# Retention values and gates of a head as a 2x2 block product with seven block products, weight sums by accumulating DMAs

## The chip, the cores and the metric

The kernel runs on one core of a Trainium2 chip. The metric is the device time of one execution in microseconds. A time is a median over runs of the same program; the profile is one further execution with the hardware profiler on.

## The reference, cut to what matters

One layer over 512 tokens with 1024 features, in float32. A normalised x is multiplied by one wide weight `w_in`; its columns are the inputs of two branches. Branch A (gated delta rule, 8 heads) is not touched. In branch B (retention, 4 heads) each head has 256 columns of queries and of keys and 512 columns of values `vb` and of gates `gb`:

```python
xn = rmsnorm(x, n_mix_pre)
proj = xn @ w_in
qa, ka, va, za, beta_logit, a_dt, qb, kb, vb, gb, gate_a, gate_b = _split_cols(proj, IN_SIZES)
...
ob = chunk_retention(qb, kb, vb)          # (q k^T * decay) v, per head
ob = rmsnorm(ob, norm_b) * silu(gb)       # per head, 512 columns
yb = ob @ w_br_b
mix = (sigmoid(gate_a) * ya + sigmoid(gate_b) * yb) @ w_out
x = x + rmsnorm(mix, n_mix_post)
x = x + rmsnorm(square(relu(rmsnorm(x, n_mlp_pre) @ w_up)) @ w_down, n_mlp_post)
```

So the values and gates of a head are one product: x (512 tokens by 1024 features) times two weight blocks of 1024 by 512.

## The kernel before, in words

Every product of float32 matrices is made of three matmuls on rounded operands, `mm3` (L78 to L83): a value is split into a rounded `hi` and a rest `lo`, and hi·hi, hi·lo and lo·hi are accumulated in one PSUM bank. x is split once, into the two tiles `xs`. Weights are split as they arrive: `weights` (L85 on) takes a block of 128 partitions by 1024 elements (two contraction tiles of 512 columns, 512 KB) by a DMA issued on SP into a tile `raw`, lets ScalarE cast it to `whi` (L100) and VectorE subtract to `wlo` (L101). `raw` has two buffers in the pool `ring`; after the first retention product two more in the pool `pb_` are used in turn (`raw_pools`). `whi` and `wlo` have three buffers each, so a block is split when the block three before it is done.

`feature_major` computes features by tokens, with weights stationary and x moving; `token_major` computes tokens by features, with x stationary and weights moving, in four PSUM banks of the tag `mm` (four banks in all), one for each 128 tokens. Each of its blocks feeds 24 matmuls.

For a head h, `retention(h)` loads a decay table (POOL), makes queries and keys and rotates them, makes the four score blocks, then the values with `token_major`, split into `vr`, and the output `o` in banks of the tag `dl`; sums of squares and `rsqrt` follow on small tiles. `gb_head` then makes the gates with `token_major`, and `gate_rows` applies tanh, a product and the row scale. After that comes a product of the branch weights with an earlier head's output: for h = 0 `ya_partial(3, ...)` and the gates of branch A into `acc`, for later heads `branch_partial` into `accb`. `gated_features` transposes `o` for the next head. After the loop the gates of branch B are applied in `accb`, and `mix` is formed from `accb` and `acc`.

The program is written in order, and a scheduler places each engine's instructions by priority and by when they are ready; the splits of weights have a higher priority (L99). Each engine and each DMA queue then executes in its own order, and waits where operands or buffers are not ready.

Of the kernel before, what the change touches and what calls it, by code (L numbers as in the profile page):

```python
# [15 lines left out]
ALU = mybir.AluOpType  # L16
# [44 lines left out]
def hybrid_block_kernel(ctx: ExitStack, tc: tile.TileContext, a: dict, out: bass.AP):  # L61
# [8 lines left out]
    raw_pools = [ring]  # L70
# [7 lines left out]
    def mm3(ps, lhs, rhs, first, last):  # L78
        lh, ll = lhs
        rh, rl = rhs  # L80
        nc.tensor.matmul(ps, lh, rh, start=first, stop=False)  # L81
        nc.tensor.matmul(ps, lh, rl, start=False, stop=False)  # L82
        nc.tensor.matmul(ps, ll, rh, start=False, stop=last)  # L83

    def weights(src, k0, nk, c0, ncols, keep=None):  # L85
# [3 lines left out]
        raw = raw_pools[i % len(raw_pools)].tile([P, 1024], F32, tag="raw", name="raw", bufs=2)  # L89
# [3 lines left out]
        )  # L93
        if keep is None:
# [4 lines left out]
        with tc.high_priority(200 if i >= 6 else 0):  # L99
# [5 lines left out]
        )  # L105

# [574 lines left out]
    with tc.tile_pool(name="pb", bufs=1) as pb_:  # L681
# [3 lines left out]
        accb = pb_.tile([P, 8, T], F32, name="accb")  # L685

        def rotary(pss, dst):
            r = [pb_.tile([P, T], F32, tag=f"ro{i}", name="ro") for i in range(4)]
# [10 lines left out]
        def retention(h):  # L699
            dec = pb_.tile([P, T], F32, tag="dec", name="dec")  # L700
            nc.gpsimd.dma_start(dec, a["c_decay"][h])
            qs, ks, vs = (
                [pb_.tile([P, n, T], F32R, tag=f"{nm}{i}", name=nm) for i in range(2)]
                for nm, n in (("qr", 2), ("kr", 2), ("vr", 4))
            )
# [3 lines left out]
            for i in range(4):  # L709
# [12 lines left out]
                sc = pb_.tile([P, T], F32, tag="sc", name="sc", bufs=2)  # L722
# [5 lines left out]
            pss = token_major(w_in, x_tile, OFF_VB + h * 512, 8)  # L728
            for t in range(4):
                nc.scalar.copy(vs[0][:, t, :], pss[t])  # L730
                nc.vector.tensor_tensor(vs[1][:, t, :], pss[t], vs[0][:, t, :], ALU.subtract)
            o = pb_.tile([P, 4, T], F32, tag="o", name="o")
            ss = pb_.tile([P, 4], F32, tag="oss", name="oss")
            sq = pb_.tile([P, T], F32, tag="osq", name="osq")
            for j in range(4):
# [11 lines left out]
                nc.scalar.activation(sq, ps, AF.Square, accum_out=ss[:, j : j + 1])  # L747
# [4 lines left out]
            return Rows(  # L752
                lambda t: [(o[:, t, :], rstd[:, t : t + 1], slice(0, T))],
                lambda t, f: o[:, t, f * P : (f + 1) * P],
            )

        def gb_head(h, rows):
            pss = token_major(w_in, x_tile, OFF_GB + h * 512, 8)
# [239 lines left out]
```

## Time and profile before

| | |
|---|---|
| median of 3 runs | 1408.81 us (1408.64 to 1409.47) |
| the profiled execution, its own time | 1407.76 us |
| its span, first to last instruction | 1406.1 us |
| TensorE busy | 1389.0 us (99%) |
| VectorE, ScalarE, GpSimd busy | 808.6, 571.6, 53.0 us |
| moved by DMA | 129.74 MB, mean 92 GB/s |

In the profile PE is TensorE's matmuls, PEld its weight loads, DVE is VectorE, ACT ScalarE, POOL GpSimd, SP SyncE; SPq and POOLq are the queues on which they issue DMAs. `mm<-whi,actT` reads: the tile `mm` written from `whi` (moving) and `actT` (stationary), where `actT` holds x. A matmul's listed duration overlaps the next one's. L101 is line 101 of the kernel.

### The profile page before, as it was taken

Reading aid. Unit: us, or ns where it says so; the run is one execution under the profiler, and the core shown is the slowest. Engines: PE = TensorE matmul, PEld = TensorE weight load, DVE = VectorE, ACT = ScalarE, POOL = GpSimd, SP = SyncE. Lnnn points to the kernel's source line nnn. Section 1 sums busy time; section 2 is a strip of 40 time slices with the busy share of each in tenths; the row PEclk is TensorE's granted clock in tenths of the full one; section 3 lists DMA queues with packets and bytes.
Section 4 is the critical chain, followed back from the end, with each engine's and each line's share of the span. In section 5 each row is a group of like instructions: output and inputs, shape, how many; then the busy total and the mean of one; then the engine's idle time right before and its main releaser. Section 6 shows DMA issues by size and latency. Waiting matters only on the chain.

```text
span 1406.1 us, 17493 instructions
## 1 busy us (share of the span) xinstructions
PE 1389.0 (99%) x6766; PEld 1140.7 (81%) x6766; DVE 808.6 (58%) x1463; ACT 571.6 (41%) x1082; POOL 53.0 (4%) x100
## 2 busy tenths in 40 slices
PE   8999999999999999999999999999999999999997
PEld 5888787878888888888888888888888888888886
DVE  5599889944755564536346455445685334344445
ACT  6778564725534233233243323323354333232331
POOL 1112300200000000000000000000000000000000
PEclk9999999999999999999999999999999999999999
DMA  5232412221331342332232232231724332323321
GB/s 158 75 93 74 118 32 75 71 79 46 90 90 45 98 143 75 96 99 83 83 97 83 82 98 75 82 97 62 239 91 136 93 102 92 103 91 105 105 75 60
DMA packets 69941, 129.74 MB, mean 92 GB/s; under 512 B 4607, under 2 KB 18065, under 8 KB 69858
## 3 DMA queue, kind: packets, MB, share of 16 engines
q1 hardware_dynamic: 66128, 119.03, 28.0%
q0 software_dynamic: 3008, 8.34, 2.2%
q8 instruction: 53, 0.87, 0.3%
q10 hardware_dynamic: 722, 1.25, 0.2%
q14 instruction: 30, 0.25, 0.1%
HBM read 124.93 MB, written 3.67 MB: 91 GB/s over the span
## 4 chain that ended last, share of the span: by engine, by line
PE 90%; DVE 5%; DMA 2%; issue 2%; ACT 1%; SPq 0%; POOL 0%; DVEq 0%; ACTq 0%; POOLq 0%
PE mm L81 26%; PE mm L83 26%; PE mm L82 26%; PE tr L179 2%; DVE c_y L367 1%; DMA raw<-in_w_in_dram 1%; PE dl L83 1%; PE dl L82 1%; PE dl L81 1%; PE dl L598 1%; PE dl L626 1%; PE dl L590 1%; DVE wlo L101 1%; PE dl L606 1%; PE dl L619 1%
## 5 line engine op out<-in xcount | busy, mean ns | idle before, releaser
L101 DVE TENSOR_TENSOR wlo<-raw,whi 128x1024 fp32r<-128x1024 f32 x208 | 254.3, 1223 | 384.6 <-ACT whi L100 384.3
L100 ACT CAST whi<-raw 128x1024 fp32r<-128x1024 f32 x208 | 218.5, 1051 | 511.8 <-PE mm L82 280.1
L82 PE MATMUL mm<-actT,whi 128*128 128x512 f32 (+1 forms) x528 | 207.7, 393 | 1.2 <-DVE actT L213 1.2
L81 PE MATMUL mm<-actT,whi 128*128 128x512 f32 (+1 forms) x528 | 206.7, 393 | 1.0 <-ACT actT L212 1.0
L83 PE MATMUL mm<-actT,wlo 128*128 128x512 f32 (+1 forms) x528 | 207.1, 392 | 0.0
L81 PE MATMUL mm<-whi,actT 128*128 128x512 f32 x472 | 185.8, 394 | 0.1
L82 PE MATMUL mm<-wlo,actT 128*128 128x512 f32 x472 | 185.3, 393 | 0.0
L83 PE MATMUL mm<-whi,actT 128*128 128x512 f32 x472 | 185.1, 393 | 0.0
L81 PEld LDWEIGHTS mm<-actT,whi 128*128 128x128 f32 x528 | 99.7, 189 | 21.3 <-ACT actT L212 1.3
L82 PEld LDWEIGHTS mm<-actT,whi 128*128 128x128 f32 x528 | 100.0, 189 | 20.4 <-DVE actT L213 1.4
L83 PEld LDWEIGHTS mm<-actT,wlo 128*128 128x128 f32 x528 | 100.0, 189 | 18.9
L81 PE MATMUL mm<-hn,whi 128*128 128x512 f32 (+1 forms) x288 | 105.6, 367 | 0.6 <-DVE r L921 0.5
L82 PE MATMUL mm<-hn,whi 128*128 128x512 f32 (+1 forms) x288 | 105.4, 366 | 0.0
L83 PE MATMUL mm<-hn,wlo 128*128 128x512 f32 (+1 forms) x288 | 105.1, 366 | 0.0
L81 PEld LDWEIGHTS mm<-whi,actT 128*128 128x128 f32 x472 | 88.6, 188 | 18.9 <-ACT c_y L365 0.5
L83 PEld LDWEIGHTS mm<-whi,actT 128*128 128x128 f32 x472 | 88.7, 188 | 18.0
L82 PEld LDWEIGHTS mm<-wlo,actT 128*128 128x128 f32 x472 | 88.7, 188 | 17.8
L81 PE MATMUL mm<-og,whi 128*128 128x512 f32 x256 | 100.4, 392 | 0.0
L82 PE MATMUL mm<-og,whi 128*128 128x512 f32 x256 | 99.6, 389 | 0.0
L83 PE MATMUL mm<-og,wlo 128*128 128x512 f32 x256 | 98.4, 390 | 0.0
L367 DVE SCALAR_TENSOR_TENSOR c_y<-c_raw,convw,c_y 128x512 f32<-128x512 f32 x96 | 70.5, 751 | 3.3 <-ACT c_y L365 2.8
L81 PEld LDWEIGHTS mm<-hn,whi 128*128 128x128 f32 x288 | 54.3, 189 | 10.3 <-DVE r L921 0.9
(286 smaller groups left out, 2075.2 us busy)
## 6 DMA issues: line engine op xcount, KB each, us to landing
raw<-in_w_in_dram SPq DMA_DIRECT2D x113, 512.0 KB, 3.7
raw<-in_w_up_dram SPq DMA_DIRECT2D x36, 512.0 KB, 3.8
raw<-in_w_down_dram SPq DMA_DIRECT2D x32, 512.0 KB, 3.7
raw<-in_w_br_a_dram SPq DMA_DIRECT2D x16, 512.0 KB, 3.7
raw<-in_w_br_b_dram SPq DMA_DIRECT2D x16, 512.0 KB, 3.7
raw<-in_w_out_dram SPq DMA_DIRECT2D x8, 512.0 KB, 4.4
x<-in_x_dram SPq DMA_DIRECT2D x4, 512.0 KB, 6.1
acc<-in_x_dram POOLq DMA_DIRECT2D x4, 512.0 KB, 4.0
```

Of the source, the lines that this page charges most:

```text
L81: nc.tensor.matmul(ps, lh, rh, start=first, stop=False)
L82: nc.tensor.matmul(ps, lh, rl, start=False, stop=False)
L83: nc.tensor.matmul(ps, ll, rh, start=False, stop=last)
L100: nc.scalar.copy(hi[:, :n], raw[:, :n])
L101: nc.vector.tensor_tensor(lo[:, :n], raw[:, :n], hi[:, :n], ALU.subtract)
L179: nc.tensor.transpose(ps, src, ident)
L367: nc.vector.scalar_tensor_tensor(y, raw[:, j : j + T], tap(j), y, ALU.mult, ALU.add)
L590: nc.tensor.matmul(ks[:, hh, :], kf[:, h0 + hh, cs], state[:, hh, :], start=True, stop=True)
L598: nc.tensor.matmul(px[:, hh, :], rt[:, nn[hh], :], vx[:, hh, :], start=True, stop=True)
L606: nc.tensor.matmul(pc[:, hh, :], kd[:, nn[hh], :], vn[:, hh, :], start=True, stop=True)
L619: nc.tensor.matmul(qs[:, hh, :], qf[:, hh, cs], prev[:, hh, :], start=True, stop=True)
L626: nc.tensor.matmul(po[:, hh, :], at[:, 4 * hh + c, :], vn[:, hh, :], start=True, stop=True)
```

## The change

Tokens are halved (t = 0, 1) and features halved (k = 0, 1), so x is a 2x2 block matrix, and the weights of values (c1) and gates (c2) of a head are one, too. Seven block products replace the eight. Four of them use sums and differences of quarters of x, made once in head 0 (`feature_sums`) and split; four use sums of weight blocks. Such a sum is a `raw` tile that is loaded once and onto which POOL issues a DMA that adds the next block; the tile is split after each step (`Sums.next`). For each half of a half's four contraction tiles there is one chain of four states, W11, + W12, + W22, + W21; two further sums of two blocks and four plain blocks are made in the `ring` pool. Two products continue in a bank after its running sum was read (`skip_group_check`), p1 is copied to SBUF by ScalarE, and six additions per head on VectorE combine them. Each weight block now feeds 12 matmuls, and a head has 14 splits and 16 block loads, 8 of them accumulating.

The gates are now made together with the values, before the head's output product; tanh and the product with the gate write the tile `gs`, and the row scale and the gate are applied after the `rsqrt`. To make room, tiles share slots: `gs` uses that of the keys, `o` that of the queries, the chains use the tag `ych`, which also serves as second pool of `raw`, and branch A's result is stored to DRAM (`ya_d`) and loaded again for the end, so that `accb` can be `acc`.

```diff
@@ mm3, weights
-    def mm3(ps, lhs, rhs, first, last):
+    def mm3(ps, lhs, rhs, first, last, more=False):
...
-        nc.tensor.matmul(ps, ll, rh, start=False, stop=last)
+        nc.tensor.matmul(ps, ll, rh, start=False, stop=last, skip_group_check=more)
...
+    class Sums:
+        def __init__(self, pool, tag, blocks):
+            self.raw = pool.tile([P, 1024], F32, tag=tag, name="raw", bufs=2)
+            self.blocks, self.n = blocks, 0
+
+        def next(self, more=1):
+            for _ in range(more):
+                src, k0, c0 = self.blocks[self.n]
+                block = src[k0 * P : (k0 + 2) * P, c0 : c0 + 512].rearrange("(k p) c -> p k c", p=P)
+                dst = self.raw.rearrange("p (k c) -> p k c", k=2)
+                if self.n:
+                    nc.gpsimd.dma_start(dst, block, accum_op=ALU.add)
+                else:
+                    nc.sync.dma_start(dst, block)
+                self.n += 1
+            return split_weights(self.raw, 1024, 2)
@@ retention heads
+        accb = acc
+        ya_d = dr.tile([P, 8, T], F32, tag="ya", name="ya_d", bufs=1)
...
+        def feature_sums():
+            full = [pb_.tile([P, 2, 4, 256], F32, tag=f"vr{i}", name="full") for i in range(2)]
+            a11, a12, a21, a22 = full[0][:, 0], full[0][:, 1], full[1][:, 0], full[1][:, 1]
+            for a, (kh, th) in ((a21, (0, 1)), (a22, (1, 1)), (a11, (0, 0)), (a12, (1, 0))):
+                h, l = quarter(kh, th)
+                nc.vector.tensor_tensor(a, h, l, ALU.add)
+            nc.vector.tensor_tensor(a22, a21, a22, ALU.subtract)
+            nc.vector.tensor_tensor(a21, a11, a21, ALU.subtract)
+            nc.vector.tensor_tensor(a11, a22, a11, ALU.subtract)
+            nc.vector.tensor_tensor(a12, a12, a11, ALU.add)
+            for i, a in enumerate((a22, a11, a21, a12)):
+                s = pb_.tile([P, 2, 4, 256], F32R, tag=f"xs{i}", name="xsum")
+                nc.scalar.copy(s[:, 0], a)
+                nc.vector.tensor_tensor(s[:, 1], a, s[:, 0], ALU.subtract)
+                quarters[f"s{i + 1}"] = [s[:, 0], s[:, 1]]
+
+        def values_and_gates(c1, c2, out1, out2):
...
+            chain = [
+                Sums(pb_, "ych", [(w_in, rows(0, ks), c1), (w_in, rows(0, ks), c2),
+                                  (w_in, rows(1, ks), c2), (w_in, rows(1, ks), c1)])
+                for ks in range(2)
+            ]
...
+            a = bank()
+            for ks in range(2):
+                product(a, "11", ks, chain[ks].next(), True)
+            p1 = [tmp("p1") for _ in range(2)]
+            for t in range(2):
+                nc.scalar.copy(p1[t], a[t])
+            for ks in range(2):
+                product(a, "12", ks, one(1, c1, ks), False)
+            for t in range(2):
+                out1(t, a[t])
+            c = bank()
+            for ks in range(2):
+                product(c, "s1", ks, chain[ks].next(), True)
+            b = bank()
+            for ks in range(2):
+                product(b, "s2", ks, chain[ks].next(), True)
+            u2 = [tmp("u2") for _ in range(2)]
+            for t in range(2):
+                nc.vector.tensor_tensor(u2[t], p1[t], b[t], ALU.add)
+            for ks in range(2):
+                w = Sums(ring, "raw", [(w_in, rows(1, ks), c2), (w_in, rows(0, ks), c2)]).next(2)
+                product(b, "s3", ks, w, False)
+            for t in range(2):
+                u3 = tmp("u3")
+                nc.vector.tensor_tensor(u3, p1[t], b[t], ALU.add)
+                out2(2 + t, c[t], u3)
+            for ks in range(2):
+                product(b, "22", ks, chain[ks].next(), False)
+            for t in range(2):
+                nc.vector.tensor_tensor(p1[t], p1[t], b[t], ALU.add)
+                out1(2 + t, p1[t])
+            for ks in range(2):
+                product(c, "s4", ks, one(1, c2, ks), False)
+            for t in range(2):
+                out2(t, c[t], u2[t])
@@ retention(h), after the scores
-            pss = token_major(w_in, x_tile, OFF_VB + h * 512, 8)
...
+            if h == 0:
+                feature_sums()
...
+            def gate(t, p, u):
+                g = gs[:, t, :]
+                nc.vector.tensor_tensor(g, p, u, ALU.subtract)
+                th = tmp("g_t")
+                nc.scalar.activation(th, g, AF.Tanh, scale=0.5)
+                nc.vector.scalar_tensor_tensor(g, th, 1.0, g, ALU.add, ALU.mult)
+
+            values_and_gates(OFF_VB + h * 512, OFF_GB + h * 512, value, gate)
...
+            for t in range(4):
+                nc.vector.scalar_tensor_tensor(
+                    o[:, t, :], o[:, t, :], rstd[:, t : t + 1], gs[:, t, :], ALU.mult, ALU.mult
+                )
@@ loop over heads and end
-            gb_head(h, rows)
...
+                    nc.gpsimd.dma_start(ya_d[:, half * 4 : half * 4 + 4, :], acc[:, half * 4 : half * 4 + 4, :])
...
+            ya.append(pb_.tile([P, 4, T], F32, tag=f"xs{2 + half}", name="ya"))
+            nc.gpsimd.dma_start(ya[half], ya_d[:, half * 4 : half * 4 + 4, :])
```

## Rows read from the trace of the kernel before

**Rows 1.** The page, parts 1 and 2: busy time by engine.

```profile
span 1406.1 us, 17493 instructions
...
PE 1389.0 (99%) x6766; PEld 1140.7 (81%) x6766; DVE 808.6 (58%) x1463; ACT 571.6 (41%) x1082; POOL 53.0 (4%) x100
```

**Rows 2.** The page, part 4: the chain that ended last, shares by engine.

```profile
PE 90%; DVE 5%; DMA 2%; issue 2%; ACT 1%; SPq 0%; POOL 0%; DVEq 0%; ACTq 0%; POOLq 0%
```

**Rows 3.** Waits of PE, whole span: total us, times, longest us.

```profile
PE dl L229 <- DVE warm L224: 1.5, 1, 1.5
PE tr L179 <- DVE actT L213: 1.5, 1, 1.5
```

**Rows 4.** Groups by line and shape, 497 to 995 us: busy us, mean ns; idle before.

```profile
L101 DVE TENSOR_TENSOR wlo<-raw,whi 128x1024 fp32r<-128x1024 f32 x82 | 100.4, 1224 | 165.7 <-ACT whi L100 165.7
L81 PE MATMUL mm<-whi,actT 128*128 128x512 f32 x256 | 99.6, 389 | 0.0
...
L83 PE MATMUL mm<-whi,actT 128*128 128x512 f32 x256 | 99.6, 389 | 0.0
...
L731 DVE TENSOR_TENSOR vr<-mm,vr 128x512 fp32r<-128x512 f32 x16 | 11.0, 688 | 4.2 <-ACT vr L730 4.2
...
L730 ACT CAST vr<-mm 128x512 fp32r<-128x512 f32 x16 | 9.4, 586 | 7.2 <-PE mm L83 7.2
```

**Rows 5.** Timeline of ACT, DVE and SP, gate stage of head 0: start, us, what.

```profile
554.84 1.05 ACT L100 CAST whi<-raw 128x1024 fp32r<-128x1024 f32 x1 [4.38 <-PE mm L83]
560.28 1.05 ACT L100 CAST whi<-raw 128x1024 fp32r<-128x1024 f32 x1 [4.39 <-PE mm L83]
...
561.37 1.22 DVE L101 TENSOR_TENSOR wlo<-raw,whi 128x1024 fp32r<-128x1024 f32 x1 [4.22 <-ACT whi L100]
...
562.62 0.37 SPq L90 DMA_DIRECT2D raw<-in_w_in_dram  x1
```

**Rows 6.** DMA issues: KB each, median us from issue to landing.

```profile
raw<-in_w_in_dram SPq DMA_DIRECT2D x113, 512.0 KB, 3.7
...
acc<-in_x_dram POOLq DMA_DIRECT2D x4, 512.0 KB, 4.0
dec<-in_c_decay_dram POOLq DMA_DIRECT2D x4, 256.0 KB, 2.9
...
rope<-in_c_rope_dram POOLq DMA_DIRECT2D x1, 512.0 KB, 5.4
...
wmlp<-in_norm_mlp_pre_dram POOLq DMA_DIRECT2D x1, 512.0 KB, 9.8
```

**Rows 7.** Windows by stage: busy us (count) per engine, clock, DMA share, GB/s.

```profile
519.00:541.00 22.00, 22.00 (x100) 18.28 (x99) 10.56 (x16) 7.81 (x14) 0.55 (x1) 1.00 0.29 86
541.00:563.00 22.00, 22.00 (x98) 18.21 (x98) 7.62 (x19) 5.78 (x10) 0.00 (x0) 1.00 0.23 70
665.00:687.00 22.00, 22.00 (x99) 18.22 (x98) 9.38 (x11) 7.83 (x14) 0.00 (x0) 1.00 0.35 108
1016.00:1018.00 2.00, 2.00 (x10) 1.62 (x11) 0.00 (x0) 0.00 (x0) 0.00 (x0) 1.00 1.03 409
```

**Rows 8.** Windows and PE timeline at the start of head 0.

```profile
497.00:508.00 11.00, 11.00 (x50) 9.13 (x49) 6.36 (x10) 2.88 (x4) 0.54 (x1) 1.00 0.72 242
508.00:519.00 11.00, 11.00 (x55) 9.31 (x55) 9.14 (x14) 3.60 (x6) 0.00 (x0) 1.00 0.38 114
...
511.23 0.39 PE L81 MATMUL mm<-whi,actT 128*128 128x512 f32 x1
...
515.32 0.40 PE L81 MATMUL dl<-qr,kr 128*128 128x512 f32 x1
...
519.25 0.40 PE L81 MATMUL mm<-whi,actT 128*128 128x512 f32 x1
```

**Rows 9.** Timeline of POOL: loads of the decay table.

```profile
520.54 0.55 POOL L701 DMA_DIRECT2D dec<-in_c_decay_dram  x1 [23.00 <-DVE sc L723]
664.08 0.55 POOL L701 DMA_DIRECT2D dec<-in_c_decay_dram  x1 [143.00 <-DVE sc L723]
```

More of the change, by code (lines that the diff above doesn't have):

```diff
@@ L69, in hybrid_block_kernel @@
     ring = ctx.enter_context(tc.tile_pool(name="ring", bufs=3))
-    raw_pools = [ring]
+    raw_pools = [(ring, "raw")]
     loads = itertools.count()
@@ L93, in weights, with split_weights @@
         )
+        return split_weights(raw, n, nk, keep, 200 if i >= 6 else 0)
+    def split_weights(raw, n, nk, keep=None, ahead=200):
         if keep is None:
@@ L98, in weights @@
             hi, lo = keep
-        with tc.high_priority(200 if i >= 6 else 0):
+        with tc.high_priority(ahead):
             nc.scalar.copy(hi[:, :n], raw[:, :n])
@@ new lines, in values_and_gates, with rows, product, bank @@
+        def values_and_gates(c1, c2, out1, out2):
+            def rows(kh, ks):
+                return 4 * kh + 2 * ks
+            chain = [
[3 more added lines that the diff above has]
+            ]
+            def product(pss, x, ks, wts, first):
+                wh, wl = wts
+                xh, xl = quarters[x]
+                for t in range(2):
+                    tt = slice(t * P, (t + 1) * P)
+                    for kk in range(2):
+                        k = 2 * ks + kk
+                        mm3(pss[t], (xh[:, k, tt], xl[:, k, tt]), (wh[:, kk, :], wl[:, kk, :]),
+                            first and k == 0, k == 3, not first)
+            def bank():
+                return [psm.tile([P, T], F32, tag="mm", name="mm") for _ in range(2)]
+            def one(kh, c, ks):
+                return Sums(ring, "raw", [(w_in, rows(kh, ks), c)]).next()
+            a = bank()
[31 more added lines that the diff above has]
+                product(c, "s4", ks, one(1, c2, ks), False)
+            for t in range(2):
+                out2(t, c[t], u2[t])
@@ L687, in rotary @@
         def rotary(pss, dst):
-            r = [pb_.tile([P, T], F32, tag=f"ro{i}", name="ro") for i in range(4)]
+            r = [tmp("ro") for _ in range(4)]
             nc.vector.tensor_tensor(r[0], pss[0], cos, ALU.mult)
@@ L701, in retention @@
             nc.gpsimd.dma_start(dec, a["c_decay"][h])
[L702 to L705, printed above, removed]
+            qs, ks = (pb_.tile([P, 2, 2, T], F32R, tag=nm, name=nm) for nm in ("qr", "kr"))
+            qs, ks = [qs[:, 0], qs[:, 1]], [ks[:, 0], ks[:, 1]]
             rotary(feature_major(w_in, xs, OFF_QB + h * 256, 256, 8), qs)
@@ L766, in hybrid_block_kernel @@
             if h == 0:
-                raw_pools.append(pb_)
-            gb_head(h, rows)
+                raw_pools.append((pb_, "ych"))
             if h == 0:
@@ L788, in hybrid_block_kernel @@
         gates = []
+        ya = []
+        for half in range(2):
+            ya.append(pb_.tile([P, 4, T], F32, tag=f"xs{2 + half}", name="ya"))
+            nc.gpsimd.dma_start(ya[half], ya_d[:, half * 4 : half * 4 + 4, :])
         for half in range(2):
             pss = gate_product(OFF_GBR, half)
-            tbt = pb_.tile([P, 4, T], F32, tag="o" if half else "tb0", name="tb")
+            tbt = pb_.tile([P, 4, T], F32, tag=f"xs{half}", name="tb")
             for f in range(4):
@@ L803, in hybrid_block_kernel @@
                 ft = half * 4 + f
-                m = accb[:, ft, :]
-                nc.vector.scalar_tensor_tensor(m, gates[half][:, f, :], 1.0, pss[f], ALU.add, ALU.mult)
-                nc.vector.tensor_tensor(m, m, acc[:, ft, :], ALU.add)
+                m = gates[half][:, f, :]
+                nc.vector.scalar_tensor_tensor(m, m, 1.0, pss[f], ALU.add, ALU.mult)
+                nc.vector.tensor_tensor(m, m, accb[:, ft, :], ALU.add)
                 nc.scalar.activation(mix[0][:, ft, :], m, AF.Copy, scale=0.5)
@@ L838, in row_tiles @@
                     for kt in range(8):
-                        if kt == 6 and pm not in raw_pools:
-                            raw_pools.append(pm)
+                        if kt == 6 and len(raw_pools) == 1:
+                            raw_pools.append((pm, "raw"))
                         kept[kt] = weights(src, krow0 + kt, 1, 0, D, keeps(kt))
```

40 lines of the change are left out of this document (20 added, 20 removed).

## The prediction

> **What bounds the kernel now.** I read the page's first two parts before anything else. TensorE is busy for 99% of the span [rows 1], at a granted clock of 1.00 in the stages in question [rows 7], so a microsecond of matmul taken away is a microsecond of time, and a microsecond for which TensorE is made to wait is lost. The chain that ended last says the same from the other side: nine tenths of it is TensorE [rows 2]. Then I asked what TensorE ever waited for: the longest single wait in the whole execution is 1.5 us, at the start [rows 3]. So there is no slack to win but matmuls, and nearly no stall that the change could remove.
>
> Next I took the stretch of the four retention heads, grouped by shape [rows 4]. The values and gates are the matmuls whose moving operand is a weight block and whose stationary operand is x: 256 on each of three lines, 768 in all, which is 4 heads x 2 products x 4 row tiles x 8 contraction tiles x 3 passes. Their duration of 389 ns is not their price, since they overlap. The price is the spacing: two casts of successive weight blocks, each released by the end of an earlier block, start at 554.84 and 560.28 us [rows 5], and 24 matmuls lie between such releases: 5.44 us / 24 = 0.2267 us each. These rows also show the rhythm around it. A cast takes 1.05 us on ScalarE, the subtraction 1.22 to 1.23 us on VectorE, and the load that may overwrite the raw block is issued 0.03 us after that subtraction ends (561.37 + 1.22, then 562.62) [rows 5]. The cast waits for TensorE, so three hi/lo buffers are the limit: a block is split when the block three before it is done, two blocks ahead of its use.
>
> The windows by stage come last [rows 7]: in the value and gate stages VectorE has 7.6 to 10.6 us of work in 22 and the DMA engines carry 70 to 108 GB/s, while elsewhere they moved 409 GB/s at a share of 1.03. Both have room, and I have to see how much of it the change uses.
>
> **Removed.** A head's values and gates are eight block products of 24 matmuls each (two row tiles, four contraction tiles, three passes); seven remain. That is 24 matmuls a head, 96 in all: 96 x 0.2267 = **21.8 us** off TensorE. Nothing covers these; the removal is certain.
>
> **Weight blocks.** Before, a block fed 24 matmuls; now it feeds 12, for 2.72 us. A head splits 14 blocks instead of 8, so ScalarE has 1.05 us and VectorE 1.23 us of splitting per 2.72 us of TensorE. With the other VectorE work of the stage (four subtractions for the values, six additions of p1, four subtractions and four products for the gates, 18 at 0.69 us from the nearest rows [rows 4]) it is 14 x 1.23 + 18 x 0.69 = 29.6 us in 168 x 0.2267 = 38.1 us, 78%. That fits, but an operation which TensorE needs at once may now stand behind a 1.23 us subtraction.
>
> **Accumulating DMAs.** Each head reads 16 blocks for 8 and adds 8 of them onto a block that is already in SBUF, from POOL. The trace holds no accumulating DMA. Three of a chain's four states come by a step that can't be overlapped: split the state, then accumulate, then split again. Count half blocks from the first product: states are used at 0 and 1, 4 and 5, 6 and 7, 10 and 11. The tight step is from 4 to 6. Block 4 can be split from the start of block 2 (buffer limit above), and block 6 is needed 4 x 2.72 = 10.9 us later. Between lie the hand-off and the two splits: 0.2 + 1.08 + 1.23 + 0.03 before the DMA and 1.08 + 1.25 + 0.1 behind it, 4.97 us. So a DMA that lands within L = **5.9 us** of its issue costs nothing; above that TensorE waits L - 5.9 once a head (the second chain is shifted by one block and has the same distance; the step from 6 to 10 has twice the time).
>
> What is L? From below, a plain 512 KB load from POOL landed in 4.0 us and 256 KB in 2.9 [rows 6], that is 1.8 us fixed and 1.1 per 256 KB. An accumulation also reads its destination; if this is as much traffic again, L is 1.8 + 4 x 1.1 = 6.2 us alone. From above, read and write one behind the other at the price of the POOL load with the same 2 KB rows beside other traffic, rope's 5.4 us [rows 6]: 10.8 us. The DMAs are not alone: in 38 us a head moves 16 blocks and reads 8 destinations, 24 x 0.524 MB, 330 GB/s against the 409 seen [rows 7], and around the tight step the accumulations for the sixth product run beside the chain's. I take 6.9 us, nearer the lower row: 1.0 us a head, **+4.0 us**, from 0 (L of 4.0) to 19.6 (L of 10.8).
>
> The Trainium skill, Collectives: The Full Stack, Part 3, says of an add inside a DMA that it is slower not for the arithmetic but because it emits two read descriptors for a chunk, both on one read ring, and so runs at half the rate of a copy. By that rule L alone would be the 6.2 us of doubled traffic and the term 4 x 0.3 = 1.2 us; no run here shows an accumulation yet.
>
> POOL's queue had little in this stretch: the next head's decay table, which waits at its head until the scores have been read, 143 us in one case [rows 9]. If it stood ahead of the chain's first accumulation it would hold that one to the end of the scores. The accumulation is free earlier (its block is split before the scores), so I expect it in front and charge nothing. The loads on SP go into slots freed 5 us and more before use.
>
> **Adding into a bank that was just read.** Before, a bank was read when its sum was complete. Now p1 is copied out by ScalarE between the first two products, and VectorE twice reads a running sum which TensorE then goes on with. The two banks alternate, so TensorE returns to the first bank 7 x 0.2267 = 1.59 us after the last matmul into it. That matmul takes 0.39 and the VectorE read 0.69 [rows 4], so it is free if VectorE is; behind a subtraction that just began it costs 0.39 + 0.69 + 1.23 - 1.59 and a hand-off of 0.1, 0.8 us. ScalarE's copy, 0.59 like the cast of a value bank [rows 4]: 0.39 + 0.59 + 1.05 - 1.59 = 0.44 at worst. Per head 0 to 2.0 us; at 78% load I take half, 1.0, **+4.0 us** over four heads (0 to 8).
>
> **Sums of x, head 0 only.** Twelve VectorE operations of the subtraction's size, 12 x 1.22 = 14.7 us, and four casts. The third product needs nine of them, 11.0 us. Values began at 511.23 us, with 3.9 us of scores in between (515.32 to 519.25) [rows 8], so it is due at 511.2 + 10.9 + 3.9 = 526.0. VectorE was idle for 4.6 and 1.9 us in the two windows before 519 [rows 8] and has some 2 us free after it, about 8 us against 11: **+3.0 us** (0 if all were fitted in, 6 if the early gaps are not used).
>
> **At nothing.** The gates are now done ahead of the output product, so the rsqrt chain of a head loses the gate product as cover; the branch product that follows, 96 matmuls or 21.8 us, covers it instead; even if each of its thirteen small operations and four row products took as long as a row operation [rows 4], 17 x 0.69 = 11.7 us, it would be done. Storing ya to DRAM and reloading it is 2 MB each way with a whole head to land in. The order inside retention moves no other matmul.
>
> **Sum.** -21.8 + 4.0 + 4.0 + 3.0 = -10.8 us. The profiled execution took 1407.76 us (span 1406.1 and 1.66 around it), giving 1397.0; the median of the runs is 1.05 us above the profiled one, so the forecast in its terms is **1398.0 us**.
>
> **Rivals.** *All hidden:* L is at most 5.9, the reads fall between the subtractions, the sums fill VectorE's gaps. VectorE's many idle stretches [rows 7] speak for it, the 330 GB/s and the 78% against. It gives -21.8, 1387.0 us.
>
> *The accumulation is late (slower):* one mechanism, the step from block 4 to block 6. For it speak that two accumulating streams run at once there and that a POOL load of 512 KB, broadcast from one row, took 9.8 us [rows 6] in traffic; against it, the 4.0 us of a plain one. With the other terms as above, the gain is gone at 4 x (L - 6.9) = 10.8, L = 9.6 us; at 10.8 us it costs 19.6 in place of 4.0, and the kernel takes 1398.0 + 15.6 = 1413.6 us.
>
> *VectorE crowds out the gain:* in a stage at 78% every read of a running sum waits in full (8.0), the sums of x are wholly late (6.0), and the splits around the accumulation slip by a further 1.0 us a head, 8.0 with the 4.0 above. Then -21.8 + 8 + 6 + 8 = +0.2, no change, 1409.0 us.
>
> **How the numbers follow.** Forecast (a part of the gain lost, 1390 to 1405) 48%; all hidden 17%; crowded, near no change 10%; accumulation late 25%. A measurement of this kernel tells about 0.2%, 2.8 us, from no change. Faster by more takes the first two, less a point where the forecast's terms run high: 64%. Within 0.2%: 10%. Slower: 26%. The range runs from all hidden, 1387, to all three unknown costs at their upper bounds, -21.8 + 19.6 + 8 + 6 = +11.8, 1420.6, rounded to 1420; outside I leave 2 in 10 for an L beyond 10.8.
>
> **What the changed profile would show.** The groups of value matmuls count 672 instead of 768, still 0.2267 us apart. POOL shows 32 accumulating DMAs; their landing time decides: below 6 us no wait of TensorE at the fourth product, above it a wait of L - 5.9 released by the hi cast or the subtraction. Waits of TensorE behind a read of a running sum should be under 0.8 us each, twelve in all. In head 0 there should be one wait of some 3 us for the sums of x. The prediction is wrong if L is 10 us or more, if the queue order on POOL holds the first accumulation behind the decay table, or if VectorE, not the DMA, releases most of TensorE's waits.

## The result, and the profile after

The changed kernel takes 1412.43 us (median of nine executions; the ratio leaves out two disturbed ones, 2356 and 2987 us, and the other seven lie between 1409.59 and 1413.29, with a median of 1411.72). The kernel before, beside it, takes 1408.37 us (1406.73 to 1409.47). The ratio is 1.0025, interval 1.0014 to 1.0036: slower by some 0.25%, or 3.4 us, where the forecast was 1398.0 us and faster. The time lies in the range, the sign is wrong. The profiled execution is the fastest of the seven, 1409.59 us against 1407.76, so the trace has 1.8 us to explain, and not the 3.4 of the medians.

The page, parts 1, 4, 5 and 6, answers to [rows 1, 2, 4, 6]:

```profile
span 1407.9 us, 17525 instructions
...
PE 1374.6 (98%) x6670; PEld 1123.7 (80%) x6670; DVE 869.4 (62%) x1539; ACT 603.9 (43%) x1118; POOL 93.3 (7%) x136
...
PE 83%; DVE 7%; DMA 6%; issue 2%; ACT 2%; POOL 0%; SPq 0%; DVEq 0%; ACTq 0%; POOLq 0%
...
raw<-in_w_in_dram POOLq DMA_DIRECT2D x32, 512.0 KB, 6.1
```

The 96 matmuls are gone (6670 for 6766). An addition lands after 6.1 us, in the lower half of what was bounded. But DMA, 2% of the chain that ended last, is now 6% of it, and TensorE is no longer busy throughout. The waits of TensorE over the whole span (total, times, longest), against [rows 3]:

```profile
PE mm L82 <- DVE u L788: 6.4, 4, 1.7
PE mm L82 <- ACT whi L105: 5.4, 5, 1.2
PE mm L83 <- DVE wlo L106: 3.1, 5, 0.8
PE dl L82 <- ACT kr L809: 2.4, 1, 2.4
```

L788 is the first read of a running sum after the fifth product (`u3`), L105 and L106 are the split, L809 casts the rotated keys. The seven products of a head are counted in the program's order: the second goes on in the first one's bank, the fourth, fifth and sixth share one, and the fifth uses the sums of two blocks. (The prediction and some expectations call these sums the sixth product's.) I laid the waits on the timeline by the distance between starts of successive matmuls: between 490 and 1000 us none of before is over 0.5 us, and in the changed kernel fifteen are, together 20.0 us beyond the normal 0.23 each. They fall in four places.

**A, ahead of the second product: 5.4 us, four times 1.35.** Timeline of PE, ACT and DVE in head 1:

```profile
669.53 0.39 PE L84 MATMUL mm<-whi,actT 128*128 128x512 f32 x1
671.10 0.73 PE L82 MATMUL mm<-whi,xsum 128*128 128x512 f32 x2 [1.18 <-ACT whi L105]
671.78 0.50 PE L82 MATMUL mm<-whi,actT 128*128 128x512 f32 x1
...
670.00 1.04 ACT L105 CAST whi<-raw 128x1024 fp32r<-128x1024 f32 x1 [0.51 <-ACT s L836]
...
671.15 1.07 ACT L769 COPY p<-mm 128x512 f32<-128x512 f32 x2
```

The first product ends at 669.53 + 0.39 = 669.92. Only then is a `whi` buffer free, and the cast starts at 670.00. The scheduler put it ahead of the copy of the finished product (`p1`, L769), so the copy begins at 671.15 and the second product at 671.78. Two matmuls of the third product were moved forward as well and wait for the same cast.

**C, ahead of the sixth product: 7.0 us, 1.7 to 1.9 a head.** Timelines of POOL, ACT, DVE and PE in head 1:

```profile
686.08 1.17 POOL L125 DMA_DIRECT2D raw<-in_w_in_dram  x1 [2.47 <-DVE wlo L106]
...
693.51 2.12 ACT L105 CAST whi<-raw 128x1024 fp32r<-128x1024 f32 x2 [3.79 <-DMA raw<-in_w_in_dram]
...
694.59 1.23 DVE L106 TENSOR_TENSOR wlo<-raw,whi 128x1024 fp32r<-128x1024 f32 x1 [3.62 <-ACT whi L105]
695.74 0.68 DVE L788 TENSOR_TENSOR u<-p,mm 128x512 f32<-128x512 f32 x1
...
694.61 0.39 PE L82 MATMUL dl<-vr,s 128*128 128x512 f32 x1
696.56 0.47 PE L82 MATMUL mm<-whi,actT 128*128 128x512 f32 x1 [1.56 <-DVE u L788]
```

Read it upwards. TensorE waits for `u3`, a VectorE operation of 0.68 us whose operand was finished by 693.19 (692.80 is the start of the last matmul into its bank, the seventh from the end of the fifth product, and 0.39 its duration). VectorE stands in front of it in a subtraction that waited 3.62 us for its cast, the cast 3.79 us for the addition issued at 686.08. The addition was in time for its own block, the second half of the sixth product: without the wait that half would start twelve matmuls after 694.84, at 697.56, and its subtraction ended at 695.82. Late is only the read that stands behind it, by the order of VectorE's queue.

**B, in the fourth product: 4.2 us.** The chain's third state is late, as the prediction's tight step had it: 0.77, 1.07 and 1.24 us between starts in heads 1 to 3, 1.06 and 1.26 in head 0.

**Head 0: 3.3 us, and a clock.** Timelines of DVE, ACT and PE, and windows (busy per engine, granted clock, DMA share, GB/s):

```profile
514.32 1.21 DVE L727 TENSOR_TENSOR full<-full 128x1024 f32<-128x1024 f32 x1
515.45 0.68 DVE L804 TENSOR_TENSOR ro<-mm,rope 128x512 f32<-128x512 f32 x1
...
515.56 1.05 ACT L733 CAST xsum<-full 128x1024 fp32r<-128x1024 f32 x1 [2.42 <-DVE full L727]
516.52 1.04 ACT L105 CAST whi<-raw 128x1024 fp32r<-128x1024 f32 x1
...
519.17 0.50 PE L82 MATMUL dl<-qr,kr 128*128 128x512 f32 x1 [2.40 <-ACT kr L809]
...
516.00:519.20 3.20, 0.80 (x5) 0.34 (x3) 3.20 (x6) 2.26 (x4) 0.00 (x0) 1.00 0.78 138
...
520.50:524.00 3.50, 3.50 (x11) 2.78 (x11) 2.73 (x4) 1.35 (x2) 1.17 (x1) 0.51 0.77 175
```

The sums of x (L726 to L733) stand between the rotary operations, so it is mainly not the third product that waits for them but the scores, which come earlier: 2.79 us between starts. The first matmuls of the third product have another 0.92. After the scores' wait the granted clock is 0.51, the lower of TensorE's two levels, for 3.4 us; at half speed that loses 1.7 us. Before, no stretch between 19 and 1401 us was below full clock.

The balance of the profiled execution: -21.8 + 5.4 + 7.0 + 4.2 + 3.3 = -1.9, + 1.7 of clock, + 1.9 in distances between 0.28 and 0.5 us (before, 44 of these add 4.6 us; now 71 add 7.8, the stretch of half clock among them), is +1.7. Compared matmul by matmul, two things outside the heads cancel. The changed kernel is already 0.8 us late at 388 us, where both kernels have run the same matmuls, after a start with 6.83 us at half clock for 3.41. And a wait of 0.95 us between starts at 1016 us of before, behind the heads, is absent. From head to head it is 98.8 to 99.45 us against 100.0 before: some 0.9 us saved of 5.44.

### The profile page after: what moved, and what is told of

It is laid out like the page before. It is cut to its first block, busy times and chain, and to the rows that moved or that the text cites. A ratio compares the mean times of both kernels' runs of the same rounds, so it can differ in the third digit from the quotient of the medians.

```text
span 1407.9 us, 17525 instructions
## 1 busy us (share of the span) xinstructions
PE 1374.6 (98%) x6670; PEld 1123.7 (80%) x6670; DVE 869.4 (62%) x1539; ACT 603.9 (43%) x1118; POOL 93.3 (7%) x136
## 3 DMA queue, kind: packets, MB, share of 16 engines
q10 hardware_dynamic: 722, 1.25, 0.2%
## 4 chain that ended last, share of the span: by engine, by line
PE 83%; DVE 7%; DMA 6%; issue 2%; ACT 2%; POOL 0%; SPq 0%; DVEq 0%; ACTq 0%; POOLq 0%
PE mm L82 24%; PE mm L84 24%; PE mm L83 24%; DMA raw<-in_w_in_dram 5%; PE tr L203 2%; DVE wlo L106 2%; ACT whi L105 1%; DVE c_y L391 1%; PE dl L622 1%; PE dl L650 1%; PE dl L83 1%; PE dl L84 1%; PE dl L82 1%; PE dl L614 1%; PE dl L630 1%
## 5 line engine op out<-in xcount | busy, mean ns | idle before, releaser
L106 DVE TENSOR_TENSOR wlo<-raw,whi 128x1024 fp32r<-128x1024 f32 x232 | 282.9, 1223 | 352.0 <-ACT whi L105 350.3
L105 ACT CAST whi<-raw 128x1024 fp32r<-128x1024 f32 x232 | 242.9, 1052 | 495.6 <-PE mm L83 286.6
L82 PE MATMUL mm<-whi,actT 128*128 128x512 f32 x312 | 124.6, 399 | 6.5 <-DVE u L788 6.4
L83 PE MATMUL mm<-wlo,actT 128*128 128x512 f32 x312 | 123.1, 395 | 0.0
L84 PE MATMUL mm<-whi,actT 128*128 128x512 f32 x312 | 123.1, 395 | 0.0
L82 PEld LDWEIGHTS mm<-whi,actT 128*128 128x128 f32 x312 | 58.6, 188 | 21.8 <-ACT whi L105 5.9
L84 PEld LDWEIGHTS mm<-whi,actT 128*128 128x128 f32 x312 | 58.6, 188 | 11.7
L83 PEld LDWEIGHTS mm<-wlo,actT 128*128 128x128 f32 x312 | 58.6, 188 | 11.4
```

The lines of the kernel that those rows point to most:

```text
L82: nc.tensor.matmul(ps, lh, rh, start=first, stop=False, skip_group_check=more)
L83: nc.tensor.matmul(ps, lh, rl, start=False, stop=False, skip_group_check=more)
L84: nc.tensor.matmul(ps, ll, rh, start=False, stop=last, skip_group_check=more)
L105: nc.scalar.copy(hi[:, :n], raw[:, :n])
L106: nc.vector.tensor_tensor(lo[:, :n], raw[:, :n], hi[:, :n], ALU.subtract)
```

## The experiments

Two theories stood at the start. **Q, the queues:** the reads of running sums (A, C) stand behind splits in ScalarE's and VectorE's queues, whatever the DMA does; order them and the time comes back. **D, the landing:** the additions land too late, and the waits are how that shows; land earlier and the time comes back. The expectations name a third, **V**: VectorE is simply too busy at 78%. Each kernel was timed beside the kernel before, in four to twelve executions. The time of a kernel varies by 2 to 6 us, so ratios are compared; the profile is one execution.

### Plain loads in place of the additions (e1_plain)

```diff
-                    nc.gpsimd.dma_start(dst, block, accum_op=ALU.add)
+                    nc.gpsimd.dma_start(dst, block)
```

> Leaves out the additions of weight blocks: POOL loads the block plainly over the raw tile, in the same order and with the same waits; TensorE's order is unchanged. The changed kernel took 1412.4 us (profiled 1409.6). Theory Q (reads of running sums stand in the queue behind a split that itself waits, so the loss is split between the buffer limit and the landing): landing falls from 6.1 to about 4.3 us, the wait at the fourth product (4 x 0.6 to 1.9, 4.2 us) and most of the wait of the sixth product's bank (4 x 1.75 = 7.0 us) go, the wait ahead of the second product (4 x 1.35 = 5.4 us, released by the end of a product and a cast, no DMA) stays: 1400 to 1403 us. Theory D (late accumulations are behind all of the 20 us of waits): all go, 1393 to 1396. Theory V (VectorE is simply too busy at 78%): its work is unchanged, 1411 to 1413.

1397.91 us, ratio 0.9927 (0.9916 to 0.9939). The wait list and the loads from POOL:

```profile
PE mm L82 <- ACT whi L105: 4.7, 4, 1.2
PE dl L82 <- ACT kr L809: 2.5, 1, 2.5
...
raw<-in_w_in_dram POOLq DMA_DIRECT2D x32, 512.0 KB, 4.2
```

Same order on TensorE, landing 4.2 us in place of 6.1: B and C are gone, A stays at 1.57 us between starts four times, head 0 stays. Neither theory has all of it: A belongs to Q, B to D, and C needs both, the order of the queue and the landing of 6 us and more. V is out: VectorE's work is the same, and some 14 us came back.

### All reads of running sums after the last product (e2_reads_late)

```diff
-            for t in range(2):
-                nc.scalar.copy(p1[t], a[t])
             for ks in range(2):
                 product(a, "12", ks, one(1, c1, ks), False)
+            for t in range(2):
+                nc.scalar.copy(p1[t], a[t])
...                                               # u2 and u3 move behind product 22
```

> Leaves out the reads of running sums in the middle: p1, u2, u3 and the gates' first operand are read only after the last product into their bank, so their values are other ones; the same instructions in number and size, accumulations as in the changed kernel. Theory Q: the waits ahead of the second product (5.4 us) and ahead of the product that follows the sixth read (7.0 us) go, 12.4 us; the wait at the fourth product (4.2 us) stays, and a late state of the chain may now show itself at its own split: 1400 to 1404 us. Theory D: a product that waited behind a read now waits for its late block instead, only the 5.4 us go: 1406 to 1408. Theory V: 1411 to 1413.

1403.42 us, 0.9964 (0.9952 to 0.9976). A and C are gone, but B has grown in head 1 (to 1.05 and 1.26 us between starts; in head 2 it shrank, to 0.58), and head 0 has a new wait of 5.5 us for a cast of the values, with half clock behind it.

### The reads ahead of the splits (e3_order)

```diff
-                nc.scalar.copy(p1[t], a[t])
+                read1 = nc.scalar.copy(p1[t], a[t]).ins
...
-                product(c, "s1", ks, chain[ks].next(), True)
+                with tc.issue_after(read1):
+                    wts = chain[ks].next()
+                product(c, "s1", ks, wts, True)
...
-                nc.vector.tensor_tensor(u3, p1[t], b[t], ALU.add)
+                read3 = nc.vector.tensor_tensor(u3, p1[t], b[t], ALU.add).ins
...
-                product(b, "22", ks, chain[ks].next(), False)
+                with tc.issue_after(read3):
+                    wts = chain[ks].next()
+                product(b, "22", ks, wts, False)
```

> Nothing left out: the split of the third product's blocks is queued behind the copy of p1 on ScalarE, and the subtraction of the last chain state behind the second read of the running sum on VectorE; no wait is added. Theory Q: order in the queues is the cause, so both waits go or shrink to 0.3 us: 12.4 us less some 2, 1401 to 1404 us. Theory D: the last state is late anyway, the wait moves to its own split: 1406 to 1409. Theory V: 1411 to 1413.

1403.48 us, 0.9959 (0.9945 to 0.9972): the order alone makes the changed kernel faster than before. Timelines of ACT and PE in head 1, and a window:

```profile
668.46 0.58 ACT L769 COPY p<-mm 128x512 f32<-128x512 f32 x1
668.94 1.05 ACT L105 CAST whi<-raw 128x1024 fp32r<-128x1024 f32 x1
...
681.50 1.99 ACT L105 CAST whi<-raw 128x1024 fp32r<-128x1024 f32 x2 [1.55 <-DMA raw<-in_w_in_dram]
...
680.01 0.50 PE L82 MATMUL mm<-whi,xsum 128*128 128x512 f32 x1 [1.09 <-ACT whi L105]
681.27 0.50 PE L83 MATMUL mm<-wlo,xsum 128*128 128x512 f32 x1 [0.76 <-DVE wlo L106]
...
681.90:685.40 3.50, 3.50 (x10) 2.72 (x9) 2.36 (x2) 1.60 (x2) 1.97 (x2) 0.51 0.58 70
```

A is gone in heads 1 to 3 (head 0 now has 2.43 us there) and C in all; head 2 has a new wait of 1.39 us between starts, for a cast of the seventh product that stands behind a cast waiting 4.72 us for a DMA. But TensorE, no longer held at A, reaches the fourth product earlier, and the chain does not: B is 1.48 + 1.26 us in head 1 for 0.77. The waits of the changed kernel had been the chain's slack. The distances over 0.5 us lose 11.6 us for 20.0; two more stretches of half clock, at 528 and 682, take back some 3.4.

### Head 0 without the sums of x (e4_nosums)

```diff
-                feature_sums()
+                for i, q in enumerate(((0, 0), (0, 1), (1, 0), (1, 1))):
+                    quarters[f"s{i + 1}"] = quarter(*q)
```

> Leaves out the sums of x in head 0 (quarters of x stand in for them, so values and gates are other ones). All theories: the wait of 2.6 us for the rotated keys and those of 0.7 and some 1 us at the third and fourth product of head 0 go, 3 to 5 us: 1408 to 1410. If VectorE's idle time had covered the sums, nothing changes: 1412.

1407.2 us, 0.9989 (0.998 to 0.9999), some 5 us below the changed kernel, which is what head 0 had lost: 3.3 of waits and 1.7 of clock. That the two agree this closely is in part luck, since the executions lie between 1403.2 and 1408.9. A, B and C stay, and in this profile one C, in head 2, is 3.43 us with half clock behind it.

### All three together (e5_floor)

The edits of e1_plain, e3_order and e4_nosums in one kernel.

> Leaves out the additions of weight blocks and the sums of x (plain loads and quarters of x stand in), and queues two splits behind the reads of running sums. If the 21.8 us are on TensorE and only the three kinds of wait ate them (late landings 11 us, reads behind a split that waits for its buffer 5.4, sums of x in head 0 3 to 5), nothing is left but the removal: 1387 to 1389 us, no wait of TensorE over 1 us in the four heads. If the higher load on VectorE, ScalarE and the DMA engines costs by itself, 1391 to 1395.

1389.48 us, 0.9876 (0.9861 to 0.9892), between the two ranges expected and nearer the first, with no distance over 0.5 us in the heads. The medians are 18.0 us apart. The profile, the fastest of four executions, has a span of 1385.5 us, 20.6 below before, but 1.0 of that was won ahead of the heads and 0.75 behind them (the wait at 1016 us). In the heads 18.8 of the 21.8 us come out. The other 3.0 are mainly distances between 0.28 and 0.5 us (66 of them add 7.1 us, for 44 and 4.6 before); four, 1.1 us together, are short waits for the copy of p1.

### Each addition twice (e8_twice)

```diff
                     nc.gpsimd.dma_start(dst, block, accum_op=ALU.add)
+                    nc.gpsimd.dma_start(dst, block, accum_op=ALU.add)
```

> Each accumulation is made twice, the second behind the first (weight sums are other ones), so a state lands about 12.2 us after the split that freed it and not 6.1. If the time from a split to the next state sets the pace, each microsecond of landing beyond 5.9 costs one a head at the fourth product, and the step to the last state, 4.97 + 12.2 against 16.3 us, some 0.9 more: 4 x 7 = 28 us, 1437 to 1443 us. If the DMA engines' throughput set it, twice the reads would cost as much at 600 GB/s wanted against 409 seen, 4 x 15 us and more: over 1460. If landing is not what counts, 1412 to 1416.

1518.11 us, 1.0785 (1.077 to 1.0799): 106 us above the changed kernel, far over the 28 us that the time from a split to the next state would cost, and in the range set for the DMA engines' throughput (over 1460). The waits, landing and one window of head 1:

```profile
PE mm L82 <- ACT whi L105: 73.0, 15, 12.7
...
raw<-in_w_in_dram POOLq DMA_DIRECT2D x64, 512.0 KB, 7.7
...
700.00:720.00 20.00, 6.84 (x26) 5.00 (x26) 2.66 (x4) 1.63 (x2) 6.60 (x7) 0.71 0.94 159
```

A head waits four times (13.08, 2.92, 3.67 and 8.15 us between starts in head 1), mostly for a cast that waits for an addition, with half clock after the long ones. An addition that is late is paid for at every step that needs one, and the DMA engines are at 0.94 in a window in which TensorE mostly stands. How much of the 106 us is the longer landing and how much the full DMA engines, this run doesn't tell.

### Third product ahead of the second (e6_swap1, e7_swap1_plain)

To give the chain back its slack, heads 1 to 3 took the product with the chain's second state first, so that the third state can be formed earlier. The second kernel is the first with plain loads.

```diff
-            for ks in range(2):
-                product(a, "12", ks, one(1, c1, ks), False)
...
-            for ks in range(2):
-                product(c, "s1", ks, chain[ks].next(), True)
-            b = bank()
+            for s1 in ((False, True) if late else (True, False)):
...
+            b = [psx.tile([P, T], F32, tag="dl", name="dl", bufs=3) for _ in range(2)]
```

> Nothing left out. In heads 1 to 3 the third product (second state of the chains) is issued ahead of the second one, in all heads the bank of the fourth, fifth and sixth product is one of the tag dl. The states are then used at half blocks 0, 2, 6 and 10, with 16.3 us between the splits of successive states and not 10.9, and two blocks lie between the first product and the one that goes on in its bank. If distance in the chain and that read are the causes, in three heads the waits ahead of the second (1.35), at the fourth (0.6 to 1.0) and behind the third read (1.8 to 1.9) go: 3 x 4.0 = 12 us, 1399 to 1402 us. If landing costs through the load on the DMA engines, no more than the 1.35 a head go: 1407 to 1410.

> As the kernel with the third product ahead of the second, with plain loads in place of accumulations (additions of weight blocks left out). If with 16.3 us between splits a landing of 6.1 us is covered, a landing of 4.2 changes only head 0: 2 to 4 us below that kernel. If landing still counts, 8 us or more below it.

With additions 1420.04 us, 1.0086 (1.0072 to 1.01), slower than either expectation; with plain loads 1399.07 us, 0.9937 (0.9924 to 0.9949). With additions: POOL's queue, three windows (the second last figure is the DMA share, the last GB/s), then DVE and PE in head 1, and the wait list:

```profile
677.74 4.87 POOL L125 DMA_DIRECT2D raw<-in_w_in_dram  x4 [5.61 <-DMA raw<-in_w_in_dram]
...
684.00:686.00 2.00, 2.00 (x10) 1.66 (x9) 0.98 (x1) 1.47 (x2) 0.00 (x0) 1.00 1.11 203
687.00:692.00 5.00, 0.36 (x2) 0.00 (x0) 1.83 (x3) 1.99 (x2) 0.00 (x0) 0.82 1.10 241
692.00:699.00 7.00, 6.86 (x20) 5.51 (x21) 2.21 (x3) 1.05 (x1) 0.00 (x0) 0.64 0.55 167
...
690.17 1.23 DVE L106 TENSOR_TENSOR wlo<-raw,whi 128x1024 fp32r<-128x1024 f32 x1 [3.32 <-ACT whi L105]
691.31 1.27 DVE L785 TENSOR_TENSOR u<-p,dl 128x512 f32<-128x512 f32 x2
...
692.14 0.77 PE L82 MATMUL dl<-whi,xsum 128*128 128x512 f32 x1 [4.77 <-DVE u L785]
...
PE dl L82 <- DVE u L785: 14.0, 3, 4.8
```

Four additions leave in a burst at 677.7, 678.7, 680.2 and 681.4 and land after 6.1, 7.7, 8.8 and 11.0 us, at 683.8, 686.5, 689.0 and 692.4: one every 2.5 to 3.4 us. TensorE stands for 5.16 us between starts, ahead of the fifth product, and then runs at half clock. But what it waits for is again a read: `u2` (L785), the first read of the fourth product's bank. Its operand was finished by 685.55 (685.16 + 0.39, the seventh matmul from the end of the fourth product). It stands behind the split of the fifth product's second block, which waited for the third addition of the burst, and VectorE was idle for 3.32 us meanwhile. The first block had been split by 686.25. So the burst made the addition late and the queue's order made TensorE wait for it early; an estimate from these rows is that with `u2` queued ahead of that split some 3 of the 5 us go. No kernel here tries it.

The same four as plain loads (674.2 to 677.8) land at 678.6, 680.4, 681.7 and 683.0, one every 1.3 to 1.7 us, the rhythm in which they were issued. The rates are read where the DMA engines are full, 203 GB/s at a share of 1.11 with additions alone (684 to 686 us above) and, in the kernel with plain loads:

```profile
678.00:680.00 2.00, 2.00 (x10) 1.65 (x9) 0.29 (x2) 1.26 (x2) 0.53 (x1) 1.00 1.00 389
```

The Trainium skill, Collectives: The Full Stack, Part 3, gives a reduce-scatter, which adds inside its DMAs, half the rate of a copy. The traces agree for this accumulating DMA into SBUF: 203 GB/s for 389.

### The order, with the sums of x behind the keys (e10_order_sums), and the swap with POOL reordered (e9_swap_pool)

```diff
+                rotated.append(nc.scalar.copy(dst[0][:, i, :], r[2 * i]).ins)    # and the subtraction
...
-                nc.scalar.copy(s[:, 0], a)
-                nc.vector.tensor_tensor(s[:, 1], a, s[:, 0], ALU.subtract)
+                with tc.issue_after(rotated[-1]), tc.issue_after(rotated[-2]):
+                    nc.scalar.copy(s[:, 0], a)
+                    nc.vector.tensor_tensor(s[:, 1], a, s[:, 0], ALU.subtract)
...
+                    self.last = nc.gpsimd.dma_start(dst, block, accum_op=ALU.add).ins
...
-                w = Sums(ring, "raw", [(w_in, rows(1, ks), c2), (w_in, rows(0, ks), c2)]).next(2)
+                with tc.issue_after(chain[1].last):
+                    w = Sums(ring, "raw", [(w_in, rows(1, ks), c2), (w_in, rows(0, ks), c2)]).next(2)
```

The last two hunks are in e9_swap_pool alone; both have the order of e3_order. Of the sums of x only the later steps are held back: the four first additions (L726) stay free, and one still runs at 512.41 us, ahead of the keys' rotary operations.

> The changed kernel with nothing left out, in the order of e3_order (the split of the chain's blocks queued behind the copy of the first product and behind u3's reads), and in head 0 the sums of x queued behind the last rotated key block on ScalarE and VectorE. If head 0's wait for the rotated keys (2.79 us between matmul starts, and a stretch of half clock after it that cost about 1.7) comes only from the sums standing ahead in the two queues: 1403.5 less 2.4 and less 1.7, so 1399 to 1401, and the gap before the first score matmul is gone. If the sums then come late for head 0's second product instead (their readers are the products on xsum), that wait moves there: 1402 to 1405, with a gap of 2 us or more before the first matmul on xsum. The fourth product's waits (2.7 us a head in heads 1 to 3) stay in either case, since they hang on the accumulating transfer's landing.

> The swap of e6_swap1 (in heads 1 to 3 the third product ahead of the second), with the sixth product's additions queued on GpSimd behind the last addition of the chain, the reads ahead of the splits as in e3_order, and the sums of x as in e10_order_sums; nothing left out. If e6_swap1's waits of 5 us a head came from GpSimd's queue (the sixth product's addition standing ahead of the chain's), they go, the first and the last of the waits stay gone as well, and what is left is up to 1.5 us a head: 1393 to 1399, below e10_order_sums. If they came from the rate of the additions in a burst (2.6 to 3.4 us apart for 512 KB each), a wait of 3 to 5 us a head stays at the third or the sixth product, with half clock after it: 1403 to 1416.

e10_order_sums: 1400.97 us, 0.9943 (0.9931 to 0.9956), the lowest time of the kernels that compute the whole layer, 8 us below the kernel before, though its interval overlaps that of e3_order. Its waits, and ACT at the second product of head 0:

```profile
PE mm L83 <- DVE wlo L106: 2.1, 3, 0.8
PE mm L82 <- ACT p L771: 2.0, 1, 2.0
PE mm L82 <- ACT whi L105: 1.6, 2, 1.3
...
PE dl L82 <- ACT kr L817: 1.2, 1, 1.2
...
524.39 1.04 ACT L735 CAST xsum<-full 128x1024 fp32r<-128x1024 f32 x1 [0.24 <-DVE full L729]
525.34 0.58 ACT L771 COPY p<-mm 128x512 f32<-128x512 f32 x1
```

The keys' wait falls to 1.56 us between starts but is not gone, and head 0 keeps 2.44 us ahead of its second product, as in e3_order, with half clock behind it. There the first product ends at 523.92 (523.53 + 0.39), but the copy of p1 stands in ScalarE's queue behind the cast of a sum of x: the same kind of wait as A, with other work in front. The time fell into the first range, but the sign named for that range, no gap ahead of the scores, did not hold; waits at B that came out smaller in this run (0.68 + 1.26 us in head 1 for 1.48 + 1.26) made up for it.

e9_swap_pool: 1444.83 us, 1.0266 (1.0247 to 1.0286), worse than both expectations. Sending the chain's additions first did not help. TensorE's longest waits are again ahead of the fifth product, 6.66 to 7.32 us between starts in heads 1 to 3:

```profile
PE dl L82 <- DVE u L789: 22.3, 4, 6.9
...
674.77 2.37 POOL L125 DMA_DIRECT2D raw<-in_w_in_dram  x2 [4.61 <-DVE wlo L106]
683.43 2.37 POOL L125 DMA_DIRECT2D raw<-in_w_in_dram  x2 [6.29 <-DVE wlo L106]
```

Two additions issued at 674.8 and 675.5 land 6.1 and 11.1 us later; those for the fifth product, held back to 687.5 and 689.3, land after 8.0 and 9.7, the first at 695.5. Its block is split from 695.59 to 697.89, and `u2` (L789) comes behind that, at 697.81. So most of this wait is the late addition, and some 2 us at its end the read behind the split. Whether the block was late by the hold or by the burst, these runs don't tell.

## Why the prediction was wrong

| step of the prediction | taken | shown |
|---|---|---|
| **Removed** | -21.8 | 18.8 us come out in the heads when no distance over 0.5 us is left (e5_floor) |
| **Accumulating DMAs**: landing L | 6.9 us | 6.1 us |
| the same: waits at the fourth product | +4.0 | +4.2 (B) |
| **Adding into a bank that was just read** | +4.0, at most 8 | +12.4 (A 5.4, C 7.0) |
| **Sums of x, head 0 only** | +3.0 | +3.3, and 1.7 of clock; 5 us by e4_nosums |
| shorter distances (0.28 to 0.5 us) | 0 | +1.9 |

*The step that failed* is "Adding into a bank that was just read". Its worst case was a read "behind a subtraction that just began", 0.8 us on VectorE and 0.44 on ScalarE. The worst case of a queue executed in order is another: the split that stands ahead may itself be waiting. For A it waits for a buffer that the just finished product has to free, so the read can't start before that product ends plus a whole cast; plain loads don't touch it (e1_plain), ordering does (e3_order). For C it waits for an addition; both an earlier landing (e1_plain) and another order (e3_order) remove it. The test named for this step, waits under 0.8 us each, failed on the trace, 1.6 to 1.7 us each at L788. It takes most of the gain: 12.4 for 4.0 is 8.4 of the 10.8 us forecast. Alone it would have left 2.4 us, and the clock and the last row, 3.6 us together, which no term had, turn the sign.

*The accumulation* went nearly as bounded. L was the 6.2 us of doubled traffic, within 0.1, not the 6.9 taken. By the half rate of the Trainium skill, Collectives: The Full Stack, Part 3, the term would have been 1.2 us. The measured 4.2 is nearer to the 4.0 taken, but by luck: L was smaller than taken, and the hand-offs were longer. In head 1 the deciding block is split at 674.88, its addition is issued at 677.49, 0.29 us after the subtraction where I took 0.03, and lands after 5.9 us; the second subtraction ends at 685.78 and TensorE goes on at 685.83, 0.54 us late where L - 5.9 gives nothing. So the late accumulation as that rival had it, at the step from block 4 to block 6 and with L of 9.6 us or more, did not happen; at L = 6.1 that step costs B alone. But the landing is half of C, and plain loads turn the sign back as ordering does (0.9927 and 0.9959). The step from 6 to 10, said to have twice the time, has 16.3 us for 10.9, one and a half times. That the wait is paid "once a head" fails with later additions: e8_twice has four waits a head.

*VectorE crowds out the gain* came nearest in time, 1409.0, partly by luck: the reads cost more than its 8.0 us (12.4), the late additions and the sums less than its 8.0 and 6.0. The sign named for it also showed: of the four longest kinds of TensorE's waits, 17.3 us, VectorE releases 9.5. Its reason, a load of 78%, isn't what happened: VectorE stood idle for 3.62 us just ahead of the subtraction that the read had to wait out.

*The sums of x* cost about the sum taken in waits, but mainly at the scores, by way of the rotary operations of the same queues, and not at the third product. The decay table held up no addition in POOL's queue that TensorE waited for: it was issued between additions (670.88 us in head 1), not ahead of the first.

*The clock* was in no term. After distances between starts of 2.79 us in the changed kernel, 2.61 and 1.48 + 1.26 in e3_order and 5.16 in e6_swap1 the granted clock was half for 3.4 to 6.8 us; after the 1.57 and about 2.0 us of A and C it stayed at full. The longer waits cost more than their length.

Left open: what makes the distances between 0.28 and 0.5 us more, in the changed kernel and in e5_floor, and how far the swap comes with `u2` queued ahead of the splits.

## What to carry to other kernels

A short operation that TensorE needs at once costs what stands ahead of it in its engine's queue, and that includes what the instruction ahead waits for: follow the releaser of the releaser before calling a wait short, and queue such an operation ahead of any work that waits for a buffer or a DMA. When the order of a program is changed, do it again for every such read: the swap failed with `u2` left behind a split. Taking work off a saturated engine uses up the slack of the chains that feed it; a chain in which a DMA, a cast and a subtraction follow one another must be measured against the shortened period, at every step, and each wait removed moves TensorE towards the next late link (A removed, B grew). An adding DMA in the place of a load counts as two loads where the DMA engines are full.

## What the runs showed of the hardware that was not expected

- An adding DMA of 512 KB into SBUF lands in 6.1 us where the plain load from the same queue takes 4.2; with the DMA engines full additions move 203 GB/s against 389 (e6_swap1, e7_swap1_plain), and in a burst one lands every 2.5 to 3.4 us.
- Its issue holds POOL for 1.17 to 1.25 us, against 0.70 to 0.74 of the plain load (e7_swap1_plain); POOL's busy time rose from 53.0 to 93.3 us.
- Beside the additions, the decay table's 256 KB landed after 5.9 us (median), for 2.9 before [rows 6]; beside plain loads it was 4.4 (e1_plain).
- Behind its longer waits TensorE ran at half the granted clock: for 3.4 us after 2.79, 6.8 after 5.16, and 10 to 13.65 after the longest in e8_twice.
